# Latent attention with the rotated query rows projected once for eight heads and carried by DMA to each head's operand

## The chip, the cores and the metric

The kernel runs on one core of one Trainium2 chip. The core has five engines that run side by side, each through its own queue of instructions: TensorE (PE, with its weight loads PEld), VectorE (DVE), ScalarE (ACT), GpSimd (POOL) and SyncE (SP, which in this kernel issues nearly all DMAs). The metric is device microseconds of one execution. The time before is 1563.23 us, the median of three runs (1559.45 to 1563.29). The profile was taken in one more execution, which took 1561.3 us.

## The reference, cut to what matters

Two decoder layers over 512 tokens of width 1024. The change touches only the mixer of the first layer, multi-head latent attention:

```python
def mla_mixer(x, pos, w_in, q_norm, w_uq, kv_norm, w_ukv, w_o):
    h = x @ w_in
    c_q, c_kv, k_rope = h[..., :512], h[..., 512:768], h[..., 768:]
    q = (rms_norm(c_q, q_norm) @ w_uq).reshape(b, s, 16, 64 + 32)
    q = concat([q[..., :64], apply_rope(q[..., 64:], pos)], -1)
    kv = (rms_norm(c_kv, kv_norm) @ w_ukv).reshape(b, s, 16, 64 + 64)
    k_nope, v = kv[..., :64], kv[..., 64:]
    k = concat([k_nope, broadcast(apply_rope(k_rope, pos))], -1)
    out = dense_causal_attention(q, k, v, 96 ** -0.5)
    return out.reshape(b, s, 1024) @ w_o

def apply_rope(x, pos):            # x1, x2: the two halves of the 32 columns
    return concat([x1 * cos - x2 * sin, x1 * sin + x2 * cos], -1)
```

So each of the 16 heads has a query of 64 plain columns and 32 rotated columns. After this mixer come cross-attention, the feed-forward block, and the whole second layer with sparse attention; they are the same in both kernels.

## The kernel before

**Precision.** Every fp32 product is computed in three matmuls on a high part and a low part of each operand: high by high, high by low, low by high (`mm3`, L115 to L118). The split is two instructions (L94 to L96): ACT casts the source to the high part (L95), and DVE, or POOL where the code says so, subtracts to get the low part (L96). Weights come in 512 KB chunks (L98 to L110): one DMA into a ring of three buffers called `raw`, then `wh` on ACT and `wl` on DVE or POOL.

**The stage of latent attention** lies from about 20 to 215 us of the span. First the four blocks of `c_q`, their norms and transposes (`rms_t`, L497 to L506), then five pieces of the values (`mla_v`), then a loop over 16 heads. In the loop (L655) head h does, in the code's order: the transposes of its probabilities (`mla_t`, L613 on PE, high parts on ACT, low parts on DVE), the scores of head h+1 (`mla_scores`: twelve matmuls, softmax pieces L399 on DVE and exponentials L405 on ACT), the projection of head h+3 (`mla_proj`), its own value pass (`mla_pv`, L632 and L633), a piece of values, and one issue of `bias_rows` (L260). The order on each engine interleaves neighbouring steps: parts of two heads are mixed, and loads of weights for later steps stand in between.

**The projection** of one head is 12 matmuls of 512 columns. The weight columns are laid out so that 128 rows come out: 64 plain rows, 32 rope rows, and the same 32 with the halves swapped. One DVE multiply (L584) by a table of ones, cosines and signed sines gives the operand `tq`, which is then split. The key operand holds the rotated key twice, so the products of plain and swapped rows add up to the rotation inside the score matmul. For each even head six more matmuls project the plain keys of a pair of heads.

**The SP queue** issues in order and stands still while the DMA at its head waits. It holds the loads of weights, and the 16 copies of `bias_rows`. Each of these writes 128 shifted rows of one head's bias for the second layer into a scratch `scr` in DRAM, and waits for the landing of the one before. The output weights `w_o` (`mla_o`, eight chunks) are loaded behind these copies, and the residual `x` (two loads of 1 MB) and the first norm's `ln_g` and `ln_b` behind them.

## Time and profile before

| | before |
|---|---|
| median of three runs | 1563.23 us |
| the profiled execution | 1561.3 us |
| its span | 1559.5 us |
| matmul busy (PE) | 1513.7 us, 97% |
| DVE / ACT / POOL busy | 64% / 42% / 20% |

A time line row gives the start in us, the duration, the engine, the line, the operation and its tiles, and in brackets the idle time of the engine just before it with what ended that idle time. Matmuls overlap in the pipeline: the duration of one row (0.39 us) is longer than the distance to the next row's start, and only that distance is what one more matmul costs.

### The profile page before, as it was taken

The page shows a single profiled execution, that of the slowest core. Times are in us where ns is not written, and L with a number is a line of the kernel's source. Part 1 is how long each engine was busy: PE and PEld are TensorE (multiplying, and loading weights), DVE is VectorE, ACT ScalarE, POOL GpSimd, SP SyncE. Part 2 cuts the span into 40 slices and gives each one's busy share as a digit, 9 for nine tenths or more (in the row PEclk, how much of TensorE's full clock was granted, in tenths as well). Part 3 has the DMA queues.
Part 4 walks back from the last instruction along what each step waited for, and adds up shares of the span by engine and source line. Part 5 has one row for each costly group of instructions (what it writes and reads, how often), then busy time and mean ns, then how long its engine had stood idle before and what let it go on. Part 6 is the DMA issues. An engine that isn't in the chain of part 4 may idle for free.

```text
span 1559.5 us, 20796 instructions
## 1 busy us (share of the span) xinstructions
PE 1513.7 (97%) x7948; PEld 1290.8 (83%) x7948; DVE 998.4 (64%) x1706; ACT 659.1 (42%) x1182; POOL 306.8 (20%) x303
## 2 busy tenths in 40 slices
PE   8999999999999999999999789999999999999997
PEld 7788778988888888888788678889888888888886
DVE  5887868454746565654668968785448466556545
ACT  4676753343233333332246489434332333333230
POOL 1322101000132331400125522010001323324002
PEclk9999999999999999999999899999999999999999
DMA  6234323322323232223241236243223132322221
GB/s 219 71 103 115 131 87 122 124 93 95 122 96 107 79 120 90 100 88 110 80 149 68 88 122 236 72 143 111 95 95 134 70 122 72 118 95 95 95 95 54
DMA packets 51320, 166.79 MB, mean 107 GB/s; under 512 B 5300, under 2 KB 11748, under 8 KB 49172
## 3 DMA queue, kind: packets, MB, share of 16 engines
q1 hardware_dynamic: 50788, 164.41, 30.8%
q8 instruction: 62, 1.02, 0.3%
q10 hardware_dynamic: 432, 1.05, 0.2%
q14 instruction: 38, 0.31, 0.1%
HBM read 161.20 MB, written 9.47 MB: 109 GB/s over the span
## 4 chain that ended last, share of the span: by engine, by line
PE 78%; DMA 8%; DVE 7%; ACT 4%; issue 1%; POOL 1%; SPq 0%; POOLq 0%; ACTq 0%; DVEq 0%
PE ps L118 24%; PE ps L116 24%; PE ps L117 24%; DMA scr<-vscr 4%; DVE t L96 2%; DVE wl L96 1%; ACT wh L95 1%; DMA raw<-in_mla_o_dram 1%; ACT t L95 1%; ACT t L405 1%; PE ps L324 1%; DVE t L954 1%; POOL sm L267 1%; PE ps L1022 1%; DVE m L953 1%
## 5 line engine op out<-in xcount | busy, mean ns | idle before, releaser
L116 PE MATMUL ps<-t,wh 128*128 128x512 f32 (+1 forms) x1264 | 459.1, 363 | 3.5 <-DVE t L96 3.4
L117 PE MATMUL ps<-t,wh 128*128 128x512 f32 (+1 forms) x1264 | 458.2, 362 | 0.9 <-DVE t L96 0.9
L118 PE MATMUL ps<-t,wl 128*128 128x512 f32 (+1 forms) x1264 | 458.1, 362 | 0.0
L95 ACT CAST wh<-raw 128x1024 fp32r<-128x1024 f32 (+2 forms) x218 | 227.4, 1044 | 470.5 <-PE ps L117 163.3
L96 DVE TENSOR_TENSOR wl<-raw,wh 128x1024 fp32r<-128x1024 f32 (+2 forms) x202 | 260.9, 1293 | 227.7 <-ACT wh L95 225.9
L116 PE MATMUL ps<-wh,t 128*128 128x512 f32 (+2 forms) x838 | 304.9, 364 | 3.8 <-DVE t L96 1.5
L118 PE MATMUL ps<-wh,t 128*128 128x512 f32 (+2 forms) x838 | 303.1, 362 | 1.0 <-DVE t L96 1.0
L117 PE MATMUL ps<-wl,t 128*128 128x512 f32 (+2 forms) x838 | 302.0, 360 | 0.0
L116 PEld LDWEIGHTS ps<-t,wh 128*128 128x128 f32 x1264 | 238.6, 189 | 41.6 <-DVE t L96 5.2
L117 PEld LDWEIGHTS ps<-t,wh 128*128 128x128 f32 x1264 | 238.6, 189 | 37.9 <-DVE t L96 1.4
L118 PEld LDWEIGHTS ps<-t,wl 128*128 128x128 f32 x1264 | 238.6, 189 | 36.7
L116 PEld LDWEIGHTS ps<-wh,t 128*128 128x128 f32 x838 | 158.8, 189 | 27.5 <-ACT t L95 1.8
L118 PEld LDWEIGHTS ps<-wh,t 128*128 128x128 f32 x838 | 158.8, 190 | 24.7 <-DVE t L96 1.4
L117 PEld LDWEIGHTS ps<-wl,t 128*128 128x128 f32 x838 | 158.9, 190 | 23.0
L95 ACT CAST t<-ps 128x512 fp32r<-128x512 f32 (+2 forms) x241 | 118.5, 523 | 132.2 <-PE ps L324 87.6
L265 POOL TENSOR_SCALAR sm<-sm 128x1 f32<-128x1 f32 x32 | 19.5, 608 | 678.9 <-DVE sm L299 635.9
L96 DVE TENSOR_TENSOR t<-ps,t 128x512 fp32r<-128x512 f32 (+2 forms) x241 | 138.7, 603 | 20.4 <-ACT t L95 19.6
L95 ACT CAST wh<-t 128x1024 fp32r<-128x1024 f32 x56 | 58.9, 1052 | 141.6 <-PE ps L117 123.6
L96 DVE TENSOR_TENSOR wl<-t,wh 128x1024 fp32r<-128x1024 f32 x56 | 71.2, 1272 | 64.9 <-ACT wh L95 63.1
L832 DVE TENSOR_TENSOR t<-ps,t 128x512 f32<-128x512 f32 x44 | 30.4, 691 | 120.4 <-PE ps L118 120.4
L96 DVE TENSOR_TENSOR t<-t,t 128x512 fp32r<-128x512 f32 (+2 forms) x113 | 84.0, 746 | 24.3 <-ACT t L95 22.1
L95 ACT CAST t<-t 128x512 fp32r<-128x512 f32 (+3 forms) x137 | 70.5, 525 | 59.6 <-POOL t L766 33.5
(176 smaller groups left out, 1687.5 us busy)
## 6 DMA issues: line engine op xcount, KB each, us to landing
raw<-in_ffn_in_dram SPq DMA_DIRECT2D x88, 512.0 KB, 3.2
t<-in_ffn_dg_dram SPq DMA_DIRECT2D x16, 1024.0 KB, 5.0
raw<-in_xa_k_dram SPq DMA_DIRECT2D x16, 512.0 KB, 3.3
raw<-in_xa_v_dram SPq DMA_DIRECT2D x16, 512.0 KB, 3.8
raw<-in_xa_q_dram SPq DMA_DIRECT2D x16, 512.0 KB, 3.9
raw<-in_xa_o_dram SPq DMA_DIRECT2D x16, 512.0 KB, 3.2
raw<-in_ffn_dl_dram SPq DMA_DIRECT2D x12, 512.0 KB, 3.2
scr<-vscr SPq DMA_DIRECT2D x16, 319.5 KB, 4.2
```

Source lines behind the costliest of these rows:

```text
L95: nc.scalar.copy(h, src)
L96: (eng or nc.vector).tensor_tensor(l, src, h.bitcast(F32), op=ALU.subtract)
L116: nc.tensor.matmul(ps, st[0], mv[0], start=start, stop=False, skip_group_check=more)
L117: nc.tensor.matmul(ps, st[0], mv[1], start=False, stop=False, skip_group_check=more)
L118: nc.tensor.matmul(ps, st[1], mv[0], start=False, stop=stop, skip_group_check=more)
L265: nc.gpsimd.tensor_scalar(a, var, scale, eps, op0=ALU.mult, op1=ALU.add)
L267: nc.gpsimd.tensor_tensor(b, a, mhalf, op=ALU.pow)
L324: nc.tensor.transpose(pt[:, k], x_of(tt)[:, 512 * n + P * k:512 * n + P * k + P], ident)
L405: nc.scalar.activation(Sx, src, AF.Exp, bias=nb, scale=scale, accum_out=self.sm[:, i:i + 1])
L832: nc.vector.tensor_tensor(sg, pu, sg, op=ALU.mult)
L953: nc.vector.max(out=m8, in_=acc[:, :n])
L954: nc.vector.match_replace(out=acc[:, :n], in_to_replace=m8, in_values=acc[:, :n], imm_value=-3e38)
```

## The change

It does the following.

- **Rope rows of eight heads at a time.** `w_uq` has six chunks instead of eight. Two of them hold the rope columns of eight heads each: the first halves of all eight as 128 rows, and the second halves as 128 rows. `mla_rope` projects each half with 12 matmuls, multiplies by cosine and sine tables on DVE, adds and splits (DVE for the first group, POOL for the second), and writes the four results to a DRAM scratch `rsc`. It runs once before the loop and once in head 1.
- **Plain rows of two heads at a time.** `mla_nope` projects a pair with 12 matmuls, splits once, and POOL copies the halves into each head's operand. A DMA of 128 KB fills the other 64 rows of that operand from `rsc` with the rotated rows, high and low.
- **Scores** stay at twelve matmuls per head with 128 rows. The operand `qa` holds the plain high rows and the rotated rows, high and low; `qz` holds the plain low rows and zeros.
- **Values.** Two pieces instead of five stand before the last transposes of `c_q`; three follow the first projections. The low part of the attention's output is taken on POOL instead of DVE.

```diff
@@ the projection
-    def mla_proj(h):
-        pr, e = h // 2, h % 2
...
-        for k in range(4):
-            mm3(pq, (wq[0][:, k, P * e:P * e + P], wq[1][:, k, P * e:P * e + P]), (cq[0][:, k], cq[1][:, k]), k == 0, k == 3)
-        tq = t2()
-        nc.vector.tensor_tensor(tq, pq, (T0, T1)[e], op=ALU.mult)
-        q = (t2(FR), t2(FR))
-        split(q[0], q[1], tq)
+    def q_block(w, c0):
+        ps = bank("a")
+        for k in range(4):
+            mm3(ps, (w[0][:, k, c0:c0 + P], w[1][:, k, c0:c0 + P]), (cq[0][:, k], cq[1][:, k]), k == 0, k == 3)
+        return ps
+    def mla_rope(o, eng):
+        w = chunk(A["w_uq"][o], (P, 4, 256))
+        x1, x2 = q_block(w, 0), q_block(w, P)
+        r1, r2, t1, t2_ = t2(), t2(), t2(), t2()
+        nc.vector.tensor_tensor(r1, x1, COS, op=ALU.mult)
+        nc.vector.tensor_tensor(r2, x1, SIN, op=ALU.mult)
+        nc.vector.tensor_tensor(t1, x2, SIN, op=ALU.mult)
+        nc.vector.tensor_tensor(t2_, x2, COS, op=ALU.mult)
+        eng.tensor_tensor(r1, r1, t1, op=ALU.subtract)
+        eng.tensor_tensor(r2, r2, t2_, op=ALU.add)
+        for i, r_ in enumerate((r1, r2)):
+            h_, l_ = t2(FR), t2(FR)
+            split(h_, l_, r_, eng)
+            nc.sync.dma_start(rsc[o, i], h_.bitcast(F32))
+            nc.sync.dma_start(rsc[o, 2 + i], l_.bitcast(F32))
+    def mla_nope(pr):
+        if pr % 2 == 0:
+            wts["q"] = chunk(A["w_uq"][2 + pr // 2], (P, 4, 256), nc.gpsimd if pr else None)
+        ps = q_block(wts["q"], P * (pr % 2))
+        qh, ql = t2(FR), t2(FR)
+        split(qh, ql, ps)
+        qa, qz = [], zq[pr % 3]
+        for e in range(2):
+            q = t2(FR)
+            rows, other = slice(64 * e, 64 * e + 64), slice(64 - 64 * e, 128 - 64 * e)
+            nc.gpsimd.tensor_copy(q[rows], qh[rows].bitcast(F32))
+            nc.gpsimd.tensor_copy(qz[e][rows], ql[rows].bitcast(F32))
+            j = 16 * ((2 * pr + e) % 8)
+            nc.sync.dma_start(q[other].bitcast(F32), rsc[pr // 4][:, j:j + 16])
+            qa.append(q)
+        qs[pr] = qa, qz
@@ scores
-            mm3(ps[:, :N], (q[0][:, ts_], q[1][:, ts_]), (k8[:, 2 * e, :N], k8[:, 2 * e + 1, :N]), True, True)
+            nc.tensor.matmul(ps[:, :N], qa[e][:, ts_], k8[:, 2 * e, :N], start=True, stop=False)
+            nc.tensor.matmul(ps[:, :N], qa[e][:, ts_], k8[:, 2 * e + 1, :N], start=False, stop=False)
+            nc.tensor.matmul(ps[:, :N], qz[e][:, ts_], k8[:, 2 * e, :N], start=False, stop=True)
@@ the value pass
-            split(oh_, ol_, of)
+            split(oh_, ol_, of, nc.gpsimd)
@@ before the loop, and the loop
-    for hv in range(5):
+    for hv in range(2):
         mla_v(hv)
...
-    qs = {0: mla_proj(0), 1: mla_proj(1)}
-    Ss = {0: mla_scores(0, qs[0])}
-    qs[2] = mla_proj(2)
+    mla_rope(0, nc.vector)
+    mla_k(0)
+    mla_nope(0)
+    mla_nope(1)
+    mla_k(1)
+    for hv in range(2, 5):
+        mla_v(hv)
+    Ss = {0: mla_scores(0)}
     for h in range(16):
         PT = mla_t(h, Ss.pop(h))
         if h + 1 < 16:
-            Ss[h + 1] = mla_scores(h + 1, qs[h + 1])
-        if h + 3 < 16:
-            qs[h + 3] = mla_proj(h + 3)
+            Ss[h + 1] = mla_scores(h + 1)
+        if h == 1:
+            mla_rope(1, nc.gpsimd)
+        if h // 2 + 2 < 8:
+            (mla_k if h % 2 else mla_nope)(h // 2 + 2)
         mla_pv(h, PT)
```

On the SP queue in the middle of the stage, before: `scr<-vscr` are the bias copies, `raw` the weight chunks.

```order
L255 DMA vscr<-t_184_870 16x128
L260 DMA scr<-vscr 128x639 x6
L106 DMA raw_1899<-in_w_uq_dram 128x1024
L260 DMA scr<-vscr 128x639
L106 DMA raw_2138<-in_w_uq_dram 128x1024
L260 DMA scr<-vscr 128x639
L676 DMA raw_2524<-in_memT_dram 128x1024
L260 DMA scr<-vscr 128x639 x4
L676 DMA raw_2534<-in_memT_dram 128x1024
L260 DMA scr<-vscr 128x639 x4
L106 DMA raw_2555<-in_mla_o_dram 128x1024
```

The same stretch of the SP queue after: `rsc<-t` are the stores of the second group's rotated rows, `t<-rsc` the loads of operands.

```order
L260 DMA scr<-vscr 128x639 x3
L581 DMA rsc<-t_233_1041 128x512
L715 DMA raw_2513<-in_memT_dram 128x1024
L582 DMA rsc<-t_234_1042 128x512
L581 DMA rsc<-t_235_1047 128x512
L582 DMA rsc<-t_236_1048 128x512
L260 DMA scr<-vscr 128x639 x2
L597 DMA t_269_1177<-rsc 64x1x512
L597 DMA t_270_1181<-rsc 64x1x512
L260 DMA scr<-vscr 128x639
L715 DMA raw_2523<-in_memT_dram 128x1024
L260 DMA scr<-vscr 128x639
```

The second group's four stores, and the first operand loads of the loop, now stand between the bias copies. Right behind the last row here stands the first `mla_o` chunk, with nine bias copies still to come; before, it stood behind all sixteen.

On ACT in the transposes of head 4 after (`t<-ps` are the four high parts of the probabilities, `wh` is the cast of that first `mla_o` chunk):

```order
L662 COPY t_298_1291<-ps_1282 64x512
L94 CAST t_303_1308<-ps_1309 128x4x64
L94 CAST t_309_1329<-ps_1324 128x512
L94 CAST wh_2546<-raw_2544 128x1024
L94 CAST t_312_1337<-ps_1333 128x384
L94 CAST t_111_598<-t_242_1094 128x512
L94 CAST t_315_1344<-ps_1341 128x256
L94 CAST t_318_1350<-ps_1348 128x128
```

The cast of the chunk stands between the first and the second high part of head 4; before, it stood in head 9's softmax, between its third and its fourth exponential.

On the SP queue at the end of the stage, before:

```order
L144 DMA t_656_2520<-in_x_dram 128x2x1024
L106 DMA raw_2645<-in_mla_o_dram 128x1024
L144 DMA t_657_2522<-in_x_dram 128x2x1024
L276 DMA t_668_2544<-in_ln_g_dram 128x1024
L277 DMA t_668_2544<-in_ln_b_dram 128x1024
L106 DMA raw_2687<-in_mla_o_dram 128x1024
```

The same place after:

```order
L143 DMA t_651_2509<-in_x_dram 128x2x1024
L597 DMA t_521_2077<-rsc 64x1x512
L597 DMA t_522_2081<-rsc 64x1x512
L143 DMA t_652_2511<-in_x_dram 128x2x1024
L276 DMA t_663_2533<-in_ln_g_dram 128x1024
L277 DMA t_663_2533<-in_ln_b_dram 128x1024
L105 DMA raw_2634<-in_mla_o_dram 128x1024
L105 DMA raw_2676<-in_mla_o_dram 128x1024
```

The fourth `mla_o` chunk, which stood between the two loads of `x`, now stands behind both and behind the norm's two rows.

## Rows read from the trace of the kernel before

**Rows 1.** The page: busy time of the engines; the chain that ended last.
```profile
PE 1513.7 (97%) x7948; PEld 1290.8 (83%) x7948; DVE 998.4 (64%) x1706; ACT 659.1 (42%) x1182; POOL 306.8 (20%) x303
PE 78%; DMA 8%; DVE 7%; ACT 4%; issue 1%; POOL 1%; SPq 0%; POOLq 0%; ACTq 0%; DVEq 0%
```

**Rows 2.** Stretches: from:to, length, busy PE, PEld, DVE, ACT, POOL, clock, DMA.
```profile
100.00:150.00 50.00, 47.59 (x279) 40.40 (x278) 41.08 (x101) 36.24 (x90) 13.79 (x22) 1.00 0.42 115
150.00:200.00 50.00, 44.28 (x260) 37.92 (x258) 40.27 (x99) 34.77 (x88) 4.20 (x15) 1.00 0.36 123
```

**Rows 3.** Time line of PE inside a projection: two neighbouring matmuls of 512 columns.
```profile
69.02 0.39 PE L116 MATMUL ps<-t,wh 128*128 128x512 f32 x1
69.24 0.39 PE L117 MATMUL ps<-t,wh 128*128 128x512 f32 x1
```

**Rows 4.** Time line of PE: first matmul of the value pass of heads 0, 1, 10, 13, 15.
```profile
78.29 0.39 PE L632 MATMUL ps<-t,t 128*128 128x512 f32 x1
...
88.75 0.39 PE L632 MATMUL ps<-t,t 128*128 128x512 f32 x1
...
173.84 0.39 PE L632 MATMUL ps<-t,t 128*128 128x512 f32 x1
...
199.92 0.50 PE L632 MATMUL ps<-t,t 128*128 128x512 f32 x1 [2.02 <-DVE t L96]
...
212.29 0.50 PE L632 MATMUL ps<-t,t 128*128 128x512 f32 x1
```

**Rows 5.** Time line of PE and DVE from the last transposes to the first scores.
```profile
56.36 0.60 PE L506 MATMUL ps<-ident,t 128*128 128x128 f32 x4
...
59.73 0.50 PE L117 MATMUL ps<-t,wh 128*128 128x512 f32 x1 [0.93 <-DVE t L96]
...
65.31 0.38 PE L116 MATMUL ps<-t,t 128*128 128x256 f32 x1
...
63.92 0.69 DVE L584 TENSOR_TENSOR t<-ps,t 128x512 f32<-128x512 f32 x1
```

**Rows 6.** Time line of POOL and DVE: two DVE multiplies of one shape, beside POOL and alone.
```profile
55.80 2.40 POOL L96 TENSOR_TENSOR wl<-raw,wh 128x1024 fp32r<-128x1024 f32 x1 [1.40 <-PE ps L118]
...
56.69 2.05 DVE L549 TENSOR_TENSOR t<-t,t 64x512 f32<-64x512 f32 x1
...
59.71 0.69 DVE L550 TENSOR_TENSOR t<-t,t 64x512 f32<-64x512 f32 x1
```

**Rows 7.** Groups by line and shape: busy us and mean ns of one.
```profile
L95 ACT CAST wh<-raw 128x1024 fp32r<-128x1024 f32 x15 | 15.7, 1050 | 9.2 <-DMA raw<-in_mla_o_dram 5.2 <-PE ps L117 3.3 <-DMA raw<-in_w_uq_dram 0.7
L96 DVE TENSOR_TENSOR wl<-raw,wh 128x1024 fp32r<-128x1024 f32 x10 | 12.0, 1222 | 5.9 <-ACT wh L95 5.9
L313 POOL TENSOR_TENSOR t<-t,t 128x512 f32<-128x512 f32 x3 | 3.8, 1283 | 2.5 <-ACT t L312 2.5
L560 POOL CAST t<-t 64x1024 fp32r<-64x1024 f32 x1 | 1.5, 1548 | 5.0 <-DVE t L557 5.0
```

**Rows 8.** The chain that ended last, in order of time: two bias copies, a weight load.
```profile
84.21 4.22 DMA scr<-vscr
...
109.44 5.79 DMA scr<-vscr
...
150.59 5.35 DMA raw<-in_mla_o_dram
```

**Rows 9.** End of the stage: an SP issue, the load it delays, PE's longest wait.
```profile
180.44 0.39 SPq L144 DMA_DIRECT2D t<-in_x_dram  x1
...
189.25 7.68 DMA raw<-in_mla_o_dram
...
190.47 0.50 PE L116 MATMUL ps<-t,wh 128*128 128x512 f32 x1 [2.15 <-DVE t L96]
```

**Rows 10.** A stretch near the program's start, columns as in rows 2.
```profile
11.60:14.90 3.30, 3.30 (x15) 3.30 (x16) 3.30 (x5) 3.30 (x4) 0.00 (x0) 0.50 0.71 264
```

**Rows 11.** DMA issues: count, KB each, median us from issue to landing.
```profile
out_dram<-t SPq DMA_DIRECT2D x6, 256.0 KB, 2.0
```

More of the change, by code (lines that the diff above doesn't have):

```diff
@@ L51, in _constants @@
     c[:, 0] = np.array(INV_FREQ, np.float32)[r % 16]
-    sw = (r >= 64) & (r % 32 < 16)
-    c[sw, 0] *= -1.0
+    c[:, 5] = np.where(r % 32 < 16, -1.0, 1.0)
     c[:64, 1] = 0.25
@@ L148, in tile_hybrid_mla_dsa_deepnorm_block @@
     vscr = dp.tile([16, GW], F32, name="vscr")
+    rsc = dp.tile([2, 4, P, S], F32, name="rsc")
     flag = cp.tile([1, 1], I32, name="flag")
@@ new lines, in mla_nope @@
+    def mla_nope(pr):
[5 more added lines that the diff above has]
+        qa, qz = [], zq[pr % 3]
+        for e in range(2):
+            q = t2(FR)
[6 more added lines that the diff above has]
+        qs[pr] = qa, qz
@@ L590, in mla_scores, with mla_k @@
+    def mla_k(pr):
+        if pr % 4 == 0:
+            wts["k"] = chunk(A["w_uk"][pr // 4], (P, 2, 512))
+        wk = wts["k"]
+        pkk = bank("a")
+        c0 = P * (pr % 4)
+        for k in range(2):
+            mm3(pkk, (wk[0][:, k, c0:c0 + P], wk[1][:, k, c0:c0 + P]), (ckv[0][:, k], ckv[1][:, k]), k == 0, k == 1)
+        k8 = K8[pr % 2]
+        split(k8[0:64, 0], k8[0:64, 1], pkk[0:64])
+        split(k8[64:128, 2], k8[64:128, 3], pkk[64:128])
+    def mla_scores(h):
         e = h % 2
@@ L591, in mla_scores @@
         k8 = K8[h // 2 % 2]
+        qa, qz = qs[h // 2]
         s01 = t2()
@@ L651, in tile_hybrid_mla_dsa_deepnorm_block @@
     OT8 = (t8(), t8())
-    qs = {0: mla_proj(0), 1: mla_proj(1)}
-    Ss = {0: mla_scores(0, qs[0])}
-    qs[2] = mla_proj(2)
+    qs = {}
+    zq = [[t2(FR) for _ in range(2)] for _ in range(3)]
+    for z in zq:
+        for e in range(2):
+            nc.gpsimd.memset(z[e][64 - 64 * e:128 - 64 * e].bitcast(F32), 0.0)
+    mla_rope(0, nc.vector)
[6 more added lines that the diff above has]
+    Ss = {0: mla_scores(0)}
     for h in range(16):
@@ L1118, in layout @@
     uq = I["mla_w_uq"][0].reshape(512, 16, 96)
-    cols = []
-    for h in range(16):
-        nope, rope = uq[:, h, :64], uq[:, h, 64:]
-        rs = [rope, rope[:, 16:], rope[:, :16]]
-        cols += [nope] + rs if h % 2 == 0 else rs + [nope]
-    uq = np.concatenate(cols, 1)
-    f["w_uq"] = uq.reshape(4, P, 8, 256).transpose(2, 1, 0, 3).reshape(8, P, 1024)
+    nope = uq[:, :, :64].reshape(512, 1024)
+    rope = uq[:, :, 64:].reshape(512, 2, 8, 2, 16).transpose(0, 1, 3, 2, 4).reshape(512, 512)
+    uq = np.concatenate([rope, nope], 1)
+    f["w_uq"] = uq.reshape(4, P, 6, 256).transpose(2, 1, 0, 3).reshape(6, P, 1024)
     ukv = I["mla_w_ukv"][0].reshape(256, 16, 128)
```

31 lines of the change are left out of this document (5 added, 26 removed).

## The prediction

> **What bounds the kernel now.** I read the page first: PE is busy for 97% of the span and holds 78% of the chain that ended last; DVE is at 64%, ACT at 42%, POOL at 20% [rows 1]. So matmul work is what counts on average. Then the stretches of the attention stage, since an average says nothing of one stage: in 100 to 150 us PE is busy for 47.59 of 50 us, in 150 to 200 for 44.28, at clock 1.00, the upper level of 2.4 GHz [rows 2]. The stage is therefore PE-bound with about 8 us of holes in these 100 us. The chain in order of time says what makes the holes: from 84 us on it is the copies `scr<-vscr`, each waiting for the last, and then the `mla_o` loads behind them [rows 8, 9]. That is the second limit: the SP queue, in order.
>
> **What the change does to PE.** It removes 48 matmuls of 512 columns: 192 for the queries before (16 heads by 12), 144 after (four rope halves and eight pairs, 12 each). A matmul costs the distance between two starts, 69.24 - 69.02, more closely 0.2265 us over a longer run [rows 3]; its row's 0.39 us would be too much. 48 x 0.2265 = 10.9 us. Scores, value passes, transposes and everything behind this stage keep their number. DVE loses per head one multiply (0.69 us [rows 5]) and one split, ACT one cast; neither bounds the stage, so that is worth little. POOL gains some 30 casts and nine splits of 128x512 (1.28 us each [rows 7]), and is at 20%, so it has room.
>
> The price is a path that was not there: project, rotate, split, store to DRAM, load, score. I follow it by five landmarks, the value passes of heads 0, 1, 10, 13, 15 [rows 4].
>
> *Start.* Two small norm loads come ahead of weight loads: 0 to 0.5 us, I take 0.2.
>
> *Up to head 0's value pass (78.29 us).* Three of five value pieces no longer cover the wait for the last norm, so PE idles until the transposes at 56.4, which DVE sets as before. Then the low parts of `cq` come at about 59.7 as they did [rows 5], or 0.4 later. 22 of the first rope group's 24 matmuls are left: 60.1 + 22 x 0.2265 = 65.1. Before, head 0's scores began at 65.31 [rows 5]. Now DVE does two multiplies, two adds, two low parts at 0.69 us and a weight split of 1.22 [rows 5, 7] that stands among them: 5.4 us, and waits for ACT's cast in between, 1 us: the last store is issued at 71.5. A store of 256 KB takes 2.0 us [rows 11]; a 512 KB weight load is ahead of it in the queue and another ahead of the operand load. At the rate of the stage's end (4.19 MB between the issue at 180.44 and the landing at 196.93, 254 KB per us [rows 9]) each is 2.1 us. 71.5 + 2.0 + 2.1 + 2.1 = 77.7, so head 0's scores begin at 77.8. Bounds: 74.5 if no weight load is in front, when PE has just finished its other work (34 matmuls and two value pieces from 65.1: 74.2), and 80 if each transfer takes the 5.35 us of a mixed one [rows 8] in part. PE thus stands still for about 3.5 us. From there PE has 7.7 us to the value pass (two sets of scores, transposes, 12 projection matmuls): 85.5. That is +7.2, between +3.9 and +9.7. Of it 2.7 is work moved forward (12 matmuls more before this point).
>
> *Head 0 to head 1 (10.46 us).* The second rope group: 24 + 6 matmuls where 18 stood. 12 x 0.2265 = +2.7.
>
> *Head 1 to head 10 (85.1 us).* Every second interval loses 12 matmuls: four of them here, 48 x 0.2265 = -10.9. Against this the SP queue. The bias copies start 5.9 us after head 0's value pass [rows 4, 8], now at 91.4. A clean one takes 4.2 us, one that shares with a weight load 5.8 [rows 8]. After three of them the queue stops for the second group's stores, which wait for a POOL row of two adds, two low parts and a weight split: 4 x 1.28 + 2.4 [rows 6, 7] = 7.5 us from 98.5, so to 106.1. Copies four to seven then are issued at about 106, 111, 116 and 120.5, and the first `mla_o` chunk right behind the seventh: it lands near 126. Its cast stands on ACT between the first and second high part of head 4, which PE reaches at about 117, and the value pass of head 4 would begin at 123.3. With 1.05 us of cast [rows 7] and the three high and low parts behind it, it begins at about 129. What is queued behind the waiting cast: three high parts, head 5's exponentials; PE waits for both. I take +5.5. Lower bound 0 (the chunk is there by 118, which needs the hold at the stores to vanish and the copies to stay clean); upper bound 9 (two shared copies more). Later loads of operands come after the sixteenth copy at about 161 and land about 166, where head 10's scores are due at 164: inside what is already lost.
>
> *Head 10 to head 15 (38.45 us).* 24 matmuls fewer, -5.4, and before's two waits of 2.15 and 2.02 us for `mla_o` chunks [rows 4, 9] could go: -7 with all of it. But the fourth chunk now stands behind 2 MB of `x`, two operand loads and 1 MB of norm rows, 3.7 MB with itself, of which the first is issued at about head 10's value pass: 3.9 / 0.254 = 15.5 us. Before, this kind of chunk took 7.68 us from its issue to its landing for the same reason [rows 9]. Its cast and its low part stand in the transposes of head 12, and the fifth chunk waits for that low part (17.8 us), lands 4 us later, and its low part (24.1 us) stands ahead of the low parts of head 13. So head 13's value pass begins 25 us after head 10's (26.08 before), and two more heads at (212.29 - 199.92) / 2 = 6.2 us [rows 4] make 37: -1.5, between -7 and +1.5.
>
> **Sum.** 0.2 + 7.2 + 2.7 - 10.9 + 5.5 - 1.5 = +3.2 us on the profiled execution's 1561.3 us: 1564.5. The median of the three runs lies 1.9 above that execution, so 1566.4, and I say 1566. All 10.9 us come off PE, and the path through DRAM and the SP queue take them back.
>
> **Rivals.**
>
> *The loads are in time (faster).* For: the middle and the end each rest on one chunk's place in the queue, and a transfer of 512 KB takes 3 to 4 us where nothing is in front. Against: the bias copies wait for each other by landing. Without the 5.5, and with half of the end's possible 5.5 back: 3.2 - 5.5 - 2.7 = -5, 1558; with all of it -7.8, 1555.5. It decides when the first `mla_o` chunk lands before about 119.
>
> *The clock falls in the new holes (slower).* Near the start PE had gaps of 1 us and then ran 15 matmuls of 256 columns at clock 0.50, the lower level of 1.2 GHz, in 3.3 us [rows 10]; at 1.00 they take half, so it cost 1.6. Against: in 150 to 200 the clock stayed at 1.00 beside a hole of 2.15 us [rows 2, 9]. The new holes are longer, 3.5 to 6 us, in four places. Three falls of 1.6 are +4.8: 1571. It decides when a hole over some 3 us is followed by a granted clock of 0.5.
>
> *DVE and POOL get in each other's way (slower).* A DVE multiply of two SBUF tiles took 2.05 us while POOL split a chunk, and 0.69 alone [rows 6]: +1.36. The new path to head 0's scores has two adds, two low parts and the chunk's split, all of two SBUF inputs, and POOL has two casts of up to 1.55 us [rows 7] there, and the copies of plain rows. If two of the five are held, +2.7; with the adds of the second group on POOL held by DVE, +1 more: 1570. The Trainium skill's page "SBUF — State Buffer" ("Who interferes with whom") says the same of the two engines: a DVE instruction with two SBUF inputs contends with a POOL instruction that reads SBUF, the later one fully blocked. By that rule the loop itself gets easier, not harder, since the splits of `tq` and of the output (two SBUF inputs) leave DVE; the trace's pair of rows agrees with the blocking.
>
> *The change does not do what it says.* The order of the instructions shows the 48 matmuls gone, so I give it nothing.
>
> **How the numbers follow.** The forecast (loads late, a small net loss, 1559 to 1571) has 0.50; loads in time 0.20; the clock 0.20; DVE and POOL 0.10. The bound for no change is 0.3%, 4.7 us, about what a measurement of this kernel can tell: 1558.5 to 1567.9. Of the forecast 0.38 lies within it, 0.12 above. Of the loads in time 0.16 lies below, 0.04 within. Of the last two 0.27 lies above, 0.03 within. Faster 0.16, same 0.45, slower 0.39. The range cuts a tenth at each end: 1555 to 1574.
>
> **What would show it.** Right: 48 matmuls less in PE's count with about the same span; PE waits of 3 us or more before head 0's scores, ended by a DMA `t<-rsc`; an ACT wait for `mla_o` of several us in head 4's transposes near 120 to 126; the value pass of head 0 near 85.5, of head 10 near 178, of head 15 near 215. Wrong: head 0's value pass before 82 (the path through DRAM is shorter than I think), no ACT wait in head 4, or head 15 before 210. Then the removed 10.9 us are a gain after all.

## The result and the profile after

| | before | after |
|---|---|---|
| median of six runs each | 1561.02 us | 1569.86 us |
| lowest and highest | 1558.69 to 1563.29 | 1567.59 to 1572.17 |
| span of the profiled execution | 1559.5 us | 1567.6 us |
| ratio after to before | | 1.0057, 95% interval 1.0045 to 1.0069 |

The change costs 8.8 us. The forecast of 1566 is 3.9 us too low, the time lies inside the range of 1555 to 1574, and the sign is that of the likeliest case. The page's first and fourth part, against [rows 1]:

```profile
PE 1513.4 (97%) x7900; PEld 1290.1 (82%) x7900; DVE 984.1 (63%) x1685; ACT 655.8 (42%) x1177; POOL 340.9 (22%) x348
...
PE 84%; DVE 6%; ACT 3%; DMA 3%; issue 2%; POOL 1%; POOLq 0%; ACTq 0%; DVEq 0%; SPq 0%
```

The 48 matmuls are gone from the count (7948 to 7900), yet PE's busy time is the same to 0.3 us. That is the first thing to read: fewer instructions, no less busy time, so the rest of them ran slower (the mean granted clock over the span is 0.988, where before has 0.994). Three stretches of after, columns as in [rows 2]:

```profile
50.00:100.00 50.00, 39.40 (x189) 32.75 (x189) 34.80 (x71) 27.72 (x63) 18.86 (x29) 0.86 0.33 108
100.00:150.00 50.00, 43.30 (x249) 36.49 (x247) 32.30 (x82) 31.83 (x78) 22.08 (x29) 0.97 0.50 141
150.00:200.00 50.00, 46.25 (x279) 39.71 (x280) 37.94 (x104) 36.15 (x97) 18.48 (x36) 1.00 0.46 135
```

In 50 to 100 us PE stands still for 10.6 of 50 us and runs at a mean clock of 0.86, in 100 to 150 it stands for 6.7 (2.4 before) at 0.97. Only 150 to 200 is better than before (46.25 busy for 44.28). The first matmuls of the value passes of heads 0, 1, 4, 10, 13 and 15 on PE's time line, to set against [rows 4]:

```profile
90.99 0.39 PE L659 MATMUL ps<-t,t 128*128 128x512 f32 x1
...
104.17 0.39 PE L659 MATMUL ps<-t,t 128*128 128x512 f32 x1
...
134.29 0.50 PE L659 MATMUL ps<-t,t 128*128 128x512 f32 x1 [1.80 <-DVE t L95]
...
184.78 0.39 PE L659 MATMUL ps<-t,t 128*128 128x512 f32 x1
...
210.06 0.50 PE L659 MATMUL ps<-t,t 128*128 128x512 f32 x1 [1.07 <-DVE t L95]
...
222.50 0.50 PE L659 MATMUL ps<-t,t 128*128 128x512 f32 x1
```

Below "P0" is the start of head 0's value pass, and so on.

| stretch | before | after | difference | forecast |
|---|---|---|---|---|
| to P0 | 78.29 | 90.99 | +12.7 | +7.4 |
| P0 to P1 | 10.46 | 13.18 | +2.7 | +2.7 |
| P1 to P10 | 85.09 | 80.61 | -4.5 | -5.4 |
| P10 to P15 | 38.45 | 37.72 | -0.7 | -1.5 |
| to P15 | 212.29 | 222.50 | +10.2 | +3.2 |

Of the 10.2 us at P15, 8.1 reach the end of the span. The three stretches behind P0 are within 1 us of the forecast; the one up to P0 is 5.3 over. How head 0's scores come to start at 80.61 stands in the chain that ended last (in order of time):

```profile
71.28 4.29 DMA rsc<-t
75.58 4.89 DMA t<-rsc
80.61 0.55 PE ps L624
```

and on PE's time line, where L502 are the last transposes of `c_q`, L624 head 0's first score matmul, and L640 a transpose of probabilities:

```profile
55.76 1.09 PE L502 MATMUL ps<-ident,t 128*128 128x128 f32 x4 [4.71 <-DVE t L499]
...
80.61 0.55 PE L624 MATMUL ps<-t,t 128*128 128x256 f32 x1 [5.68 <-DMA t<-rsc]
...
110.82 0.52 PE L640 MATMUL ps<-ident,t 128*128 128x128 f32 x3 [3.26 <-DVE t L95]
```

The store, the load and a PE that has nothing to do for 5.68 us in between. The third row is a wait in head 2's transposes that the forecast did not have. The clock in six stretches of after (columns as in [rows 2]):

```profile
75.00:80.60 5.60, 0.00 (x0) 0.03 (x1) 2.66 (x6) 2.25 (x4) 3.99 (x7) 0.81 0.44 138
80.60:85.00 4.40, 4.39 (x16) 4.00 (x17) 1.80 (x7) 1.80 (x6) 0.00 (x0) 0.50 0.28 106
85.00:88.00 3.00, 2.93 (x20) 2.42 (x19) 0.98 (x4) 2.04 (x6) 0.69 (x3) 0.96 0.08 32
110.82:115.96 5.14, 5.14 (x28) 4.26 (x28) 4.87 (x15) 3.69 (x12) 2.25 (x5) 1.00 0.82 233
134.30:138.00 3.70, 2.89 (x12) 2.33 (x13) 3.55 (x12) 2.11 (x8) 2.77 (x4) 0.79 0.33 80
203.00:207.00 4.00, 4.00 (x16) 3.92 (x17) 2.62 (x11) 3.55 (x10) 0.39 (x2) 0.50 0.39 131
```

PE is idle for 5.6 us and then runs 16 matmuls at 0.50, the lower level of 1.2 GHz; the stretch behind them is back near 1.00. Behind the 3.26 us at head 2 the clock stayed at 1.00 (fourth row), and the 0.50 from 203 us on has no such hole ahead of it: the waits there are 1.71, 1.17 and 0.74 us, and PE is busy for 1.70 of the 4.00 us from 199 to 203.

The second row shows one thing more. From 80.60 to 85.00 us only the six operand loads are under way, and the 16 DMA engines are busy for 0.28 of the time, at 106 GB/s: that is the time of four to five of the sixteen. Each of these loads reads four blocks of 16 rows of `rsc`. That the four blocks are the reason was not tested by itself.

ACT's time line shows what it stood at in heads 2 and 4:

```profile
105.17 0.62 ACT L94 CAST t<-t 128x512 fp32r<-128x512 f32 x1 [1.32 <-POOL t L576]
108.72 0.62 ACT L94 CAST t<-t 128x512 fp32r<-128x512 f32 x1 [2.46 <-POOL t L577]
132.22 1.04 ACT L94 CAST wh<-raw 128x1024 fp32r<-128x1024 f32 x1 [4.40 <-DMA raw<-in_mla_o_dram]
```

The first two are high parts of the second rope group: they wait for POOL's adds (L576, L577), and head 2's high parts are queued behind them on ACT, for which PE waits 3.26 us. The third is the wait for the `mla_o` chunk in head 4 that was forecast. The SP queue around that chunk:

```profile
97.14 8.83 SPq L260 DMA_DIRECT2D scr<-vscr  x3
106.06 0.54 SPq L581 DMA_DIRECT2D rsc<-t  x1
...
111.53 5.54 SPq L260 DMA_DIRECT2D scr<-vscr  x2
117.18 1.23 SPq L597 DMA_DIRECT2D t<-rsc  x2
120.97 0.56 SPq L260 DMA_DIRECT2D scr<-vscr  x1
...
125.67 0.54 SPq L260 DMA_DIRECT2D scr<-vscr  x1
126.30 0.55 SPq L105 DMA_DIRECT2D raw<-in_mla_o_dram  x1
```

Three bias copies, the hold at the second group's stores, four more copies, and the chunk behind the seventh: the order that the forecast had, 5.8 us later, because the copies begin after head 0's value pass and that came later.

### The profile page after: what moved, and what is told of

Read it like the earlier page. It is cut to its first block, busy times and chain, and to the rows that moved or that the text cites. A ratio compares the mean times of both kernels' runs of the same rounds, so it can differ in the third digit from the quotient of the medians.

```text
span 1567.6 us, 20800 instructions
## 1 busy us (share of the span) xinstructions
PE 1513.4 (97%) x7900; PEld 1290.1 (82%) x7900; DVE 984.1 (63%) x1685; ACT 655.8 (42%) x1177; POOL 340.9 (22%) x348
## 4 chain that ended last, share of the span: by engine, by line
PE 84%; DVE 6%; ACT 3%; DMA 3%; issue 2%; POOL 1%; POOLq 0%; ACTq 0%; DVEq 0%; SPq 0%
PE ps L115 25%; PE ps L117 25%; PE ps L116 25%; DVE t L95 1%; DVE wl L95 1%; ACT t L94 1%; ACT t L405 1%; DMA scr<-vscr 1%; ACT wh L94 1%; PE ps L324 1%; PE ps L1061 1%; POOL sm L267 1%; DVE sm L295 1%; PE ps L640 1%; DMA t<-scr 1%
## 5 line engine op out<-in xcount | busy, mean ns | idle before, releaser
L115 PE MATMUL ps<-t,wh 128*128 128x512 f32 (+1 forms) x1248 | 453.6, 364 | 1.0 <-DVE t L95 0.7
L116 PE MATMUL ps<-t,wh 128*128 128x512 f32 (+1 forms) x1248 | 452.6, 363 | 0.0
L117 PE MATMUL ps<-t,wl 128*128 128x512 f32 (+1 forms) x1248 | 452.0, 362 | 0.0
L95 DVE TENSOR_TENSOR wl<-raw,wh 128x1024 fp32r<-128x1024 f32 (+1 forms) x203 | 262.7, 1296 | 226.7 <-ACT wh L94 225.1
L115 PEld LDWEIGHTS ps<-t,wh 128*128 128x128 f32 x1248 | 236.1, 189 | 39.2 <-DVE t L95 3.1
L116 PEld LDWEIGHTS ps<-t,wh 128*128 128x128 f32 x1248 | 236.1, 189 | 36.4 <-DVE t L95 0.7
L94 ACT CAST t<-ps 128x512 fp32r<-128x512 f32 (+4 forms) x249 | 122.3, 527 | 132.1 <-PE ps L324 87.9
L95 DVE TENSOR_TENSOR t<-ps,t 128x512 fp32r<-128x512 f32 (+4 forms) x249 | 144.0, 606 | 43.6 <-ACT t L94 42.7
L94 ACT CAST t<-t 128x512 fp32r<-128x512 f32 (+2 forms) x125 | 63.1, 516 | 57.5 <-POOL t L805 33.5
L405 ACT ACTIVATE t<-t,sm 128x128 f32<-128x128 f32 (+3 forms) x128 | 71.3, 559 | 29.7 <-DVE sm L399 29.4
```

Of the source, the lines that this page charges most:

```text
L94: nc.scalar.copy(h, src)
L95: (eng or nc.vector).tensor_tensor(l, src, h.bitcast(F32), op=ALU.subtract)
L115: nc.tensor.matmul(ps, st[0], mv[0], start=start, stop=False, skip_group_check=more)
L116: nc.tensor.matmul(ps, st[0], mv[1], start=False, stop=False, skip_group_check=more)
L117: nc.tensor.matmul(ps, st[1], mv[0], start=False, stop=stop, skip_group_check=more)
L405: nc.scalar.activation(Sx, src, AF.Exp, bias=nb, scale=scale, accum_out=self.sm[:, i:i + 1])
```

## The experiments

The theory after the result: the path through DRAM (5.3 us more than in the sum) and the two things at which the loop stands, ACT behind POOL at head 2 and the chunk behind the bias copies at head 4, give the removed PE work back. Rivals: the clock alone; DVE and POOL; PE work that was worth nothing to begin with. All ratios are to the kernel before on the same chip; differences to after are differences of the ratios times 1561 us. Every landmark P is read from one profiled execution. The last transposes of `c_q` begin between 54.95 and 55.76 us in after and in two kernels with the same code up to far behind them, so a difference of up to about 1 us at a landmark says little.

### The second rope group before the loop

```diff
     mla_k(1)
+    mla_rope(1, nc.vector)
...
-        if h == 1:
-            mla_rope(1, nc.gpsimd)
```

> The second rope group is projected before the loop, right after the plain projections, and its adds and splits run on DVE; the rest is the changed kernel. Theory (the loss is PE standing still: 5.7 us before head 0's scores, and 3.3 us at 110.8 us where ACT waits for POOL's adds): 24 matmuls (5.4 us) now fill the hole, PE keeps its clock, and both waits go; head 0's value pass stays near 89 to 91 us, head 1's comes about 5.4 us earlier after it (7.8 us apart instead of 13.2), and the kernel gets 8 to 12 us faster than the changed one, that is 0 to 3 us faster than before. Rival (the time is lost in the number of DMAs and their order on the SP queue, wherever the matmuls stand): head 0's scores start 5 us later instead, since the second group's chunk and stores are in front, and the gain stays under 4 us.

1565.29 us, ratio 1.0006 [0.9996, 1.0015]: 8.0 us faster than after, level with before. The second group's matmuls fill the hole (PE waits 2.07 us before head 0's scores, at 81.02), and P0 to P1 is 7.74 us in place of 13.18, but P0 itself does not come earlier (92.61): the loads are issued at 76.84, 1.3 us later, the wait ends with a weight split on POOL that had itself waited for an operand load, and the clock is 0.72 from 81 to 85 us, against the expectation that PE would keep it. Head 2's wait is gone. What stays, from PE's and from ACT's time line at head 4:

```profile
129.28 0.80 PE L659 MATMUL ps<-t,t 128*128 128x512 f32 x1 [4.18 <-DVE t L95]
...
218.01 0.50 PE L659 MATMUL ps<-t,t 128*128 128x512 f32 x1
```

```profile
127.21 1.04 ACT L94 CAST wh<-raw 128x1024 fp32r<-128x1024 f32 x1 [6.79 <-DMA raw<-in_mla_o_dram]
```

The heads before come earlier, the chunk less so, and the wait grows from 1.80 to 4.18 us. No other edit brought more; the next one comes close (6.9 us, with overlapping intervals).

### Operand loads that wait for no store

```diff
-            nc.sync.dma_start(q[other].bitcast(F32), rsc[pr // 4][:, j:j + 16])
+            nc.sync.dma_start(q[other].bitcast(F32), rsc[pr // 4][:, j:j + 16] if pr == 7 else rs0)
```

> The operand loads of heads 0 to 13 read a small DRAM scratch that was written long before, not the rotated rows; stores stay. So nothing waits for a store to land, with the same number and size of DMAs; the rotated rows are thus left out of the scores of these heads. Theory (the way through DRAM, store landed and then load, is the price at the start): the load is issued right behind the last store, at about 71.6 instead of 75.6, head 0's scores start near 76.5 instead of 80.6, the hole behind which the clock fell shrinks to about 2 us and the clock stays at 1.00; head 0's value pass near 84 to 85 instead of 91.0, and the kernel 4 to 7 us faster than the changed one (the later waits may keep some of it). Rival (the load is late because weight chunks are in front of it in the queue): scores still start after 79, and the gain is under 2 us.

1565.77 us, 1.0013 [1.0003, 1.0023]: 6.9 us faster than after. The loads are issued at 72.25 instead of 75.58, PE's hole is 1.30 us and ends with a POOL copy, the clock stays at 1.00, and P0 comes at 86.28, 4.7 us earlier. 3.3 us of this is the earlier issue, so that is what waiting for the store cost the load; most of the rest fits the clock (1.2 us, by the dummy matmuls below). The edit changes a second thing: these loads read one block of 64 rows, and from 75 to 76 us they keep the DMA engines busy throughout, at 379 GB/s. Yet they land no sooner after their issue (4.0 to 5.6 us, median 4.8), with a store and two weight loads among them. Head 4 takes part of it back again: its wait is 3.76 us (1.80 in after).

### The second group's adds and low parts on DVE

```diff
-            mla_rope(1, nc.gpsimd)
+            mla_rope(1, nc.vector)
```

> The changed kernel with the second group's adds and low parts on DVE instead of POOL. Theory (ACT stands at its cast of the rotated rows until POOL has done add, chunk split, add, and holds head 2's probabilities behind it): the wait of 3.3 us at 110.8 us goes, the second group's stores leave some 5 us earlier, so that the bias copies and the first output-weight chunk at 132 us come some 4 us earlier too: 3 to 6 us faster than the changed kernel. Rival (DVE is as much in the way: four more instructions of 0.69 us in front of head 2's low parts): head 2's value pass gains less than 1.5 us and the kernel less than 2 us.

1572.83 us, 1.0060 [1.0041, 1.0080]: no gain, as the rival said. PE's time line of this kernel at head 2:

```profile
109.56 0.52 PE L640 MATMUL ps<-ident,t 128*128 128x128 f32 x3 [2.06 <-DVE t L95]
```

The wait fell from 3.26 to 2.06 us, so POOL's slow row was part of what ACT stood at (its casts now wait 1.99 us for DVE's add); but head 4's wait rose from 1.80 to 3.70, and P4 came at 134.95 (134.29 in after). While the chunk holds head 4, what is saved at head 2 is not saved.

### Dummy matmuls in the hole

```diff
+    fill = bank("a")
+    for _ in range(22):
+        nc.tensor.matmul(fill, cq[0][:, 0, 0:P], cq[0][:, 1], start=True, stop=True)
     Ss = {0: mla_scores(0)}
```

> The changed kernel with 22 extra matmuls of 512 columns (5.0 us, result unused) between the last value piece and head 0's scores, where PE stood still for 5.7 us. Theory (the clock falls to 0.50 behind that hole and costs about 2.4 us of scores, plus what waits for them): head 0's scores start at 80.6 as before, but run at clock 1.00, and head 0's value pass comes at 88 to 88.7 instead of 91.0; the kernel is 1.5 to 2.5 us faster although PE does 5 us more work. Rival (the hole costs nothing beyond itself, DVE and ACT set the pace of head 0): head 0's value pass stays at 91 and the time within 1 us.

1571.21 us, 1.0043 [1.0029, 1.0058]: some 2.2 us faster than after, with the two intervals overlapping. The hole is 0.56 us, the clock 1.00 from 75 to 91 us, and head 0's value pass begins 9.16 us after its first score matmul, where after takes 10.38. So the fall to 1.2 GHz costs 1.2 us at P0, not the 2.2 that 4.4 us at half speed suggest: part of it lies in a wait that is there anyway (1.07 us for a DVE low part in this kernel). At P15 nothing of it is left (222.65, in after 222.50). The clock fell at another place instead, behind the same wait of 3.26 us at head 2 that left it at 1.00 in after (columns as in [rows 2]):

```profile
107.98:114.64 6.66, 6.66 (x28) 5.59 (x28) 4.97 (x15) 3.79 (x12) 2.23 (x5) 0.74 0.61 210
```

So this run prices one fall at P0, and does not show what the clock costs in all.

### The bias table and its copies moved to the feed-forward block

In after, in before, and together with the early second group, the table and the 16 copies were taken out of the attention stage.

```diff
-    table = bias_table()
-    next(table)
...
-        if h == 0:
-            next(table)
-        else:
-            bias_rows(h - 1)
-    bias_rows(15)
+    late = list(range(16))
...
             for j in range(j0, j1, 2):
+                for _ in range(2):
+                    if late:
+                        bias_rows(late.pop(0))
```

> The changed kernel with the bias table and its 16 copies to DRAM moved out of the attention stage to the first layer's feed-forward block; all else as changed. Theory (the first output-weight chunk lands at 132 us because it stands behind seven bias copies that wait for each other): the chunk is there before head 4 needs it, the ACT wait of 4.4 us goes, heads 3 to 4 take 7 to 7.5 us instead of 11.2, and the loads of operands never wait; 3.5 to 6 us faster than the changed kernel, if the feed-forward block has room for the copies. Rival (the chunk waits for its buffer, which the split of a weight chunk on POOL frees, not for the copies): heads 3 to 4 stay above 10 us apart and the gain is under 1.5 us.

> The kernel before with the same move of the bias table and copies to the feed-forward block. It prices the copies in the old order, where the chain that ended last ran through them from 84 to 150 us but PE's waits behind them were 1 us each. Theory (in the old order the copies cost little, since only the first output-weight chunk waits behind them, in head 9): 0.5 to 2 us faster than before, heads 8 to 9 1.2 us closer. Rival (the copies were the bound of the old stage, as the chain by itself would say): 5 us or more faster.

> Both at once: the second rope group before the loop on DVE, and the bias copies in the feed-forward block. With the early group alone the value passes of heads 3 and 4 moved apart to 13.5 us (7.3 without a wait), because the bias copies now came later against the heads. Theory (the two causes are apart and add up): heads 3 to 4 take 7.3 us, all five landmarks keep the gain, and the kernel is 10 to 14 us faster than the changed one, 3 to 6 us faster than before. Rival (another wait takes their place, at the loads of x and the output weights at the end of the stage): less than 9 us faster than the changed one.

All three were expected to be faster and are slower than the kernel before, but the times do not decide between theory and rival, since all three lose in the block that now has the copies: PE is busy for 86.92, 86.84 and 87.34 of the 100 us from 450 to 550, where before has 100.00. P15 decides, since it lies ahead of this block:

| kernel | copies in the stage | P15 | ratio of time |
|---|---|---|---|
| before | yes | 212.29 | 1 |
| before, copies out | no | 209.04 | 1.0066 [1.0042, 1.0091] |
| after | yes | 222.50 | 1.0057 [1.0045, 1.0069] |
| after, copies out | no | 220.88 | 1.0118 [1.0100, 1.0137] |
| after, second group early | yes | 218.01 | 1.0006 [0.9996, 1.0015] |
| after, both | no | 210.31 | 1.0066 [1.0048, 1.0084] |

Taking the copies out of after brings 1.6 us, moving the second group 4.5, both 12.2: twice the sum. (With the copies out the last transposes came 1.1 us later, at 56.84 for 55.76; counted from there it is 2.7, 4.3 and 12.0.) With the group early, the wait at head 4 grew by 2.4 us (4.18 for 1.80): there the second hold hides part of the gain. Without the copies there is no wait for the chunk in head 4, but the wait of head 2 is still there (PE's time line of after with the copies out, and a stretch with columns as in [rows 2]):

```profile
111.03 0.88 PE L640 MATMUL ps<-ident,t 128*128 128x128 f32 x3 [3.21 <-DVE t L95]
...
111.03:118.81 7.78, 7.78 (x27) 6.67 (x28) 4.97 (x15) 3.84 (x12) 2.21 (x5) 0.62 0.37 133
```

This wait did not grow (3.21 for 3.26), but behind it the clock is 0.62, where after has 1.00, and P1 to P2 takes 14.38 us for 11.79. So in this kernel it is a fall of the clock that goes with the 2.6 us, and not a longer wait.

Even with both holds gone the change is not ahead of before on the same terms (210.31 against 209.04, and equal ratios of time). The stretches of these two kernels say where it stands. P0 is 15.2 us later (93.11 for 77.96); the 36 matmuls that now stand ahead of it are 8.2 of these, and 7.0 are left for the new path and its waits. P0 to P1 is 2.7 us shorter and P1 to P10 10.3 (73.14 for 83.39), close to what the 12 and 48 matmuls missing there are worth (2.7 and 10.9). P10 to P15 is only 1.0 shorter, for 24 matmuls (5.4). So up to head 10 the removed PE work pays once both holds are gone; the start and the end of the stage take it back.

### 48 matmuls less in the kernel before, with and without the copies

This asks what PE work is worth here at all, without any path through DRAM.

```diff
-        for k in range(4):
-            mm3(pq, (wq[0][:, k, P * e:P * e + P], wq[1][:, k, P * e:P * e + P]), (cq[0][:, k], cq[1][:, k]), k == 0, k == 3)
+        for k in range(3):
+            mm3(pq, (wq[0][:, k, P * e:P * e + P], wq[1][:, k, P * e:P * e + P]), (cq[0][:, k], cq[1][:, k]), k == 0, k == 2)
```

> The kernel before with each head's projection summed over three of its four blocks of the contraction: 16 x 3 = 48 matmuls of 512 columns fewer, nothing else; part of the projection is thus left out. It prices the removed matmuls by themselves, without the way through DRAM. Theory (PE bounds the loop, so they are worth their 10.9 us, less what the holes at the chunks take back): 8 to 11 us faster than before. Rival (DVE, ACT and the SP queue are close behind, so that fewer matmuls only turn into waits): less than 5 us faster.

1559.89 us, 0.9978 [0.9965, 0.9990]: 3.4 us for 48 matmuls, where 48 x 0.2265 is 10.9, so the rival's number. PE's time line of this kernel around head 9, and then ACT's:

```profile
145.71 0.39 PE L632 MATMUL ps<-t,t 128*128 128x512 f32 x1
...
157.58 1.12 PE L613 MATMUL ps<-ident,t 128*128 128x128 f32 x4 [9.50 <-ACT t L405]
...
165.84 0.39 PE L632 MATMUL ps<-t,t 128*128 128x512 f32 x1
```

```profile
155.87 1.05 ACT L95 CAST wh<-raw 128x1024 fp32r<-128x1024 f32 x1 [10.04 <-DMA raw<-in_mla_o_dram]
```

Head 8's value pass begins at 145.71 (154.30 in before: 8.6 us gained); head 9's at 165.84 (165.11 in before: all of it lost). In between PE stands for 9.50 us for an exponential that is queued on ACT behind the cast of the first `mla_o` chunk, and this chunk, behind the 16th copy, is issued at 150.10 (150.59 in before, [rows 8]). The chain of copies has its own clock, and PE gets ahead of it in vain.

The next three kernels spread the copies over the first layer's feed-forward block, two heads at a time, each step with its own small table. They pay for it there (from 450 to 850 us PE is busy for about 373 of 400 us at clock 0.92), so again only the stage, and the pair with and without the 48 matmuls, can be compared.

```diff
-    def bias_table():
+    def bias_step(v):
...
+                if i == 0 and late and j:
+                    bias_step(late.pop(0))
```

> As the run with the early second group and the late copies, but the copies are spread over the feed-forward block: eight small tables for two heads each, one at every second hidden block, so that two copies at most stand together. In the run with the copies in bulk the attention stage ended 12 us earlier than in the changed kernel (head 15's value pass at 210.3 instead of 222.5), and a hole of 13 us opened at 450 to 550 us where the copies stood between the weight chunks. Theory (the hole came from the clumps alone): the stage keeps its 12 us, the hole goes, and the kernel is 1 to 4 us faster than before and about 11 us faster than the changed one. Rival (any copy in the feed-forward block costs its 4 us there): slower than before by 5 us or more.

> The kernel before with the bias copies spread in the same way. With the copies in bulk its stage ended 3.2 us earlier than before (head 15's value pass at 209.0 instead of 212.3). Theory: 2 to 4 us faster than before. Rival (the spread tables cost about what the stage gains): within 1.5 us of before.

> The kernel before with 48 projection matmuls left out (three of four blocks of the contraction, so part of the projection is missing) and the bias copies spread over the feed-forward block. With the copies in the stage, leaving the 48 out brought 3.4 us, and ACT stood 9.5 us before head 9 for the first output-weight chunk behind the sixteenth copy. Theory (the copies are a fixed clock of some 66 us, and matmuls taken from PE before its end come back as a wait): without the copies the 48 matmuls are worth 7 to 10 us, so 9 to 13 us faster than before. Rival (DVE and ACT bound the loop as closely as PE does): less than 6 us faster than before.

| kernel | P15 | median | ratio |
|---|---|---|---|
| before, copies spread | 207.53 | 1636.39 | 1.0457 [1.0442, 1.0473] |
| the same with 48 matmuls less | 199.59 | 1627.55 | 1.0409 [1.0395, 1.0424] |
| after with the second group early, copies spread | 209.90 | 1635.99 | 1.0454 [1.0432, 1.0475] |

With the copies out of the stage the 48 matmuls are worth 7.9 us at P15 and 7.5 to 8.8 in time; with the copies in it, nothing at P15 (212.75 for 212.29). The price of the spread was foreseen far too low. PE's waits from 450 to 850 us of the third kernel (total us, times, longest) name part of it:

```profile
PE ps L248 <- DMA t<-in_onehot_dram: 11.7, 3, 6.9
PE ps L116 <- DVE wl L95: 9.0, 8, 2.3
PE ps L115 <- ACT wh L94: 6.6, 8, 1.2
```

PE waits there for the small table loads that now stand in the SP queue among the weights (11.7 us), and for weight parts that come late behind them.

### The table and the copies earlier

An attempt at a version that beats both: the second group early, and the table ahead of head 0's scores, so that the copies begin while PE waits.

```diff
+    next(table)
     Ss = {0: mla_scores(0)}
...
-        if h == 0:
-            next(table)
-        else:
-            bias_rows(h - 1)
-    bias_rows(15)
+        bias_rows(h)
```

> The change with its second rope group before the head loop (as in the run that moved mla_rope(1)), and the bias table computed ahead of head 0's scores, with each head's bias copy one head earlier in program order. Nothing is left out. Theory (the chain of bias copies and the mla_o chunk behind it set the stage, and the hole before head 0's scores is free room): the table's matmuls fall into that hole, the copies begin some 10 to 15 us earlier, and the wait of 4.2 us ahead of head 4's value pass shrinks below 2 us; head 15's value pass at about 214 (218.0 with the rope group alone moved), so 1561 to 1563, 0.998 to 0.999 of before. Rival (the chunk comes behind as many more copies as start earlier): the wait at head 4 stays at 4 us or moves to head 3 or 5, head 15 at 217 to 219, ratio 1.000 to 1.002.

1569.42 us, 1.0031 [1.0021, 1.0041]: 3.9 us slower than with the second group alone. From PE's time line, and the SP queue of this kernel:

```profile
135.26 0.80 PE L659 MATMUL ps<-t,t 128*128 128x512 f32 x1 [11.19 <-DVE t L95]
...
222.04 0.50 PE L659 MATMUL ps<-t,t 128*128 128x512 f32 x1
```

```profile
90.08 4.92 SPq L260 DMA_DIRECT2D scr<-vscr  x2
95.08 1.19 SPq L597 DMA_DIRECT2D t<-rsc  x2
99.40 22.78 SPq L260 DMA_DIRECT2D scr<-vscr  x6
...
125.98 0.56 SPq L260 DMA_DIRECT2D scr<-vscr  x1
126.59 0.58 SPq L105 DMA_DIRECT2D raw<-in_mla_o_dram  x1
```

The copies start 8.2 us earlier (90.08 for 98.31), but now nine of them, not six, stand ahead of the chunk. It is issued at 126.59 instead of 120.98, and head 4 waits 11.19 us instead of 4.18 (5.6 of these 7.0 by the later issue, 1.0 because head 3 came earlier, 114.72 for 115.74). The theory expected a gain, so it is wrong; it is the rival's mechanism, stronger than its price. Over all kernels with the copies in the loop, P4 follows the issue of the chunk. The issue follows how many copies stand ahead of the chunk and, among the four kernels with seven, when the first one starts:

| kernel | copies ahead | first copy | chunk issued | P4 | P4 minus issue |
|---|---|---|---|---|---|
| second group early | 6 | 98.31 | 120.98 | 129.28 | 8.3 |
| loads without a wait | 7 | 92.38 | 122.95 | 131.54 | 8.6 |
| dummy matmuls | 7 | 94.22 | 124.24 | 133.09 | 8.9 |
| second group on DVE | 7 | 96.36 | 125.89 | 134.95 | 9.1 |
| after | 7 | 97.14 | 126.30 | 134.29 | 8.0 |
| table early | 9 | 90.08 | 126.59 | 135.26 | 8.7 |

## Why the prediction was right or wrong

**PE's saving.** 48 matmuls are gone, as worked out. That their 10.9 us come off the path only where nothing else holds the stage was right: the two pairs on the kernel before show 7.9 us at P15 without the copies and none with them.

**The start (forecast +7.4, measured +12.7): the step that failed.** Up to the issue of the load the sum holds: the last store was put at 71.5 and went out at 71.28; store and the weight load ahead were to end at 75.6, and the first operand load was issued at 75.58. The failing term is the next one. A load of 128 KB behind a weight load of 512 KB was given 2.1 us, the bytes of the weight load at the stage's rate, and it took 4.89. The upper bound of 80 for head 0's scores was passed as well (80.61). The sum had priced the bytes ahead in the queue and nothing for the load itself, its own bytes and its landing: the store had been read off a row [rows 11], the load had no row and got none. The Trainium skill's page "DMA: Bandwidth & Descriptors" (section "Anatomy of one DMA — SWDGE (gpsimd) path", so of another issuing path than SP's here) gives each DMA about 2.0 us besides its bytes. By that page the load would be estimated at 2.1 + 2.0 = 4.1, nearer to the 4.89 measured; the trace agrees with the direction. It does not tell a fixed part from slow bytes: the weight load's bytes have moved by about 77 us (328 GB/s in the half us before it, 53 in the one behind), and from 78.50 to 80.50 the DMA engines are busy for 0.26, at 97 GB/s, with operand loads alone. The second part of the miss is from the scores to P0: 10.38 us where 7.7 were put. The dummy matmuls split it: at clock 1.00 it is 9.16, so 1.5 us were work and short waits that the sum left out, and 1.2 us the clock.

**The clock, a rival (given 0.20).** Its condition came true: granted clock 0.50 at 80.6 behind a hole of 5.68 us, and at 55.76, where transposes that took 0.60 us in [rows 5] take 1.09 behind a hole of 4.71. Its bound on the hole did not hold: the clock stayed at 1.00 behind 3.26 us at head 2, and fell to 0.50 at 203 us behind waits of at most 1.71. Of its price, 1.2 us are shown at P0; filling the hole at 80 us brought about 2 us in time, not clear of the noise, and nothing at P15, where the clock had fallen elsewhere. The fall at 55.76 left the last store where it was forecast (71.28 for 71.5). So the clock is a share of the loss; how large it is over the whole stage is not shown.

**DVE and POOL, a rival (given 0.10).** A DVE row of two SBUF inputs beside POOL's weight split shows the blocking again. First this row in after; then the same row in the run with the table early, where POOL was only writing zeros; then POOL's time line in after:

```profile
56.21 2.77 DVE L546 SCALAR_TENSOR_TENSOR t<-t,cst,t 64x512 f32<-64x512 f32 x1
...
55.23 0.75 DVE L546 SCALAR_TENSOR_TENSOR t<-t,cst,t 64x512 f32<-64x512 f32 x1
```

```profile
55.82 2.62 POOL L95 TENSOR_TENSOR wl<-raw,wh 128x1024 fp32r<-128x1024 f32 x1 [1.78 <-ACT wh L94]
```

DVE's row ends at 58.98 in after, half a us after POOL's at 58.44. But before had this too [rows 6], and the last store was not late: no loss at P15 was traced to it.

**Head 0 to head 1.** +2.7 forecast, +2.72 measured.

**Head 1 to head 10 (-5.4 forecast, -4.5 measured).** The ACT wait for the chunk in head 4 is where it was put, 4.40 us long, with the chunk behind the seventh copy. But that the size is near is partly luck. The forecast put 5.5 us at head 4; PE's wait there is 1.80, and the clock is 0.79 in 134.3 to 138. Another 3.26 us went at head 2, in a wait that the sum did not have: it named POOL's row of adds and low parts as what holds the stores in the SP queue, and did not ask what ACT has queued behind the two casts inside that row. In the run with the adds on DVE, 1.2 us less wait at head 2 came back as 1.9 us more at head 4. With both holds gone this stretch is 10.3 us shorter than in the kernel before without its copies, near the 10.9 that the sum took off for the matmuls.

**Head 10 to head 15 (-1.5 forecast, -0.7 measured).** Right within 1 us. Two figures of this step do not add up: 25 and twice 6.2 are 37.4, not 37, so its own terms give -1.1; and 5.4 with the two waits of 2.15 and 2.02 would be -9.6, not -7. (The upper bound of the start has a slip too: 80 and 7.7 make +9.4, not +9.7.) In the eight other kernels with the change this stretch takes 37.0 to 38.1 us whatever came before it, which fits the forecast's reason, loads behind `x` and the norm rows that do not care for the heads' 24 matmuls; no run took these loads away, so that is argued and not shown.

**The signs that were named.** A PE wait over 3 us ended by `t<-rsc`: 5.68. The ACT wait in head 4: there, at 128 to 132 instead of 120 to 126. P0 near 85.5, P10 near 178, P15 near 215: 90.99, 184.78, 222.50, late by 5.5, 6.8 and 7.5 us: most of it is there at P0.

**What stays open.** Of the 10.2 us at P15 and at the second layer's first transposes (L324, 253.6 for 243.4), 8.5 are left at the last of these (1216.8 for 1208.3); what gave back 1.7 in between was not followed. The 48 matmuls taken from before with the copies in place show nothing at P15 of the one profiled execution and 3.4 us in the medians; where these lie was not found either.

## What to carry to other kernels

Before crediting a removed matmul, ask what else in the stage has its own clock: here a chain of DMAs, each waiting for the last, with a weight chunk behind them, gave a saving of 10.9 us of PE work a worth of nothing at the stage's end in one arrangement and of 7.9 us in another, and two such holds brought 1.6 and 4.5 us when they were removed one at a time, and 12.2 together. A round trip through DRAM is a store's landing and a load's landing, each priced on its own and behind what is in the queue (4.29 + 4.89 us here for 256 and 128 KB, the load with only about a quarter of the DMA engines busy), so the producer must be that far ahead of its reader; moving the second rope group ahead of the loop gave back 8.0 of the 8.8 us. When a wait is added to an in-order engine, list what is queued behind it on every engine of that row, not only on the queue that one has in mind.

## What the runs showed of the hardware

- A load of 128 KB from DRAM to SBUF, issued 1.25 us after a weight load of 512 KB, landed 4.89 us after its issue; the store of 256 KB before it took 4.29 with a weight load in front.
- Behind an idle stretch of 5.6 us PE ran 16 matmuls at a granted clock of 0.50 for 4.4 us. The length of the wait alone does not tell: 2.15 us left the clock at 1.00 in before [rows 2, 9], 2.07 was followed by 0.72 over 4 us with the second group early; 3.26 at head 2 left it at 1.00 in after and was followed by 0.74 in the run with dummy matmuls; and in after 0.50 came behind waits of 1.71, 1.17 and 0.74 us, with PE busy for 1.70 of the 4.00 us from 199 to 203.
- Six operand loads of four blocks of 16 rows, alone under way, kept the 16 DMA engines busy for 0.28 of the time at 106 GB/s; loads of the same size from one block of 64 rows kept them busy throughout, at 379 GB/s from 75 to 76 us of the run without the wait.
- Copies that were moved among steady weight loads cost more than they did in the stage: 16 copies in a clump took 13 us of PE's time in 100 us, and spread with eight small tables some 70 us over the block (1636 for 1565 us).
